# Moving small state-space steps earlier and later around a matmul stream: f and A two blocks ahead, C behind other pairs, scan tables among the W coefficients, one coefficient group behind the scan

## The chip, the cores and the metric

The kernel runs on one core of one Trainium2 chip. The metric is the device time of one execution in microseconds; with it stands the profile of one execution, whose span is the time from the first to the last recorded event of the core.

## The reference

One decoder layer on 512 tokens of width 1024, in float32:

```
h = rms_norm(x) * norm_w
u, z_s, q, k, v, z_a, r_s, r_a = split(h @ w_in)          # w_in: 1024 x 9216
y_s = ((S5(u) glu) * silu(z_s)) @ w_ssm_out               # state-space branch
y_a = (dilated_attention(q, k, v) * silu(z_a)) @ w_attn_out
out = x + (sigmoid(r_s) * y_s + sigmoid(r_a) * y_a) @ w_o
```

The state-space branch has 64 groups of 16 channels with 64 complex states each. Per group, with `dt = exp(log_dt)` and `a = exp(lam * dt)`:

```
f  = (a - 1) / lam ;  bb = f * b
state[t] = a * state[t-1] + bb @ u[t]                     # complex, diagonal
y[t] = Re(c @ state[t]) + d_skip * u[t]
g = gelu(y);  S5 = g * sigmoid(g @ w_glu)
```

## The kernel before

**The matmul stream.** Every large product is done as three matmuls on split operands (high part times high part, high times low, low times high). A weight tile `w_raw` is fetched by a DMA of SyncE's queue (SP), ScalarE (ACT) makes its high part `w_hi` (L250), VectorE (DVE) makes its low part `w_lo` (L252). There are two raw buffers and three of each part, and a tile is prepared two units before it is used. A unit of the projection (`cm_unit`) takes one weight tile of 128 columns: 8 slices of the contraction, 3 matmuls of 128x512 each, so 24 matmuls. Two slices, six matmuls, are one *block*, and each unit of this kind has four blocks.

**The order.** All TensorE (PE) instructions are tied in the order in which the program text traces them. The other engines' queues are filled by the framework's scheduler, which takes instructions as they become ready in its own simulation, those traced first ahead of others; at run time each queue is then strictly in that order. `tc.issue_after(ins)` puts the instructions of its block behind `ins` on their engine's queue.

**Work woven into the stream.** The list `events` names for each small step the block in whose front it is traced. Block 0 is the first of unit u3; W0 = 16, K0B = 49, V0B = 74 and Y0 = 88 are marks in it. The steps, in their order:

- `f_turn` turns `pw` (f in slot 8, a in slot 0, computed on DVE, last written at L543 and L547) onto the partitions by 16 small matmuls into `ftp`. ACT copies them to `fT` (L576) and `AT` (L577). DVE makes f times b (L578 to L581) and doubles the powers of a in `AT` (L590 to L593). GpSimd (POOL) copies the top power to `A4` (L595 to L597).
- `w_unit(j)`, eight of them, three blocks apart from W0: six DVE instructions of `coef` (L422 to L424) fill one of two buffers in the tile `ab`, eight transposes bring it to `wps`, ACT copies that to `W`.
- `x_pair(i)`, four of them, at W0+5, 11, 17 and 23: 64 small matmuls per unit, of `W` with u, into `xps`; ACT copies them into `Xs` (L465, L466), the inputs of all steps of the scan.
- `ca_load(j)`, `ca_turn(j)`, `ca_coef(j)`, for eight chunks: the rows of c are loaded to `cn` (two buffers), turned by eight matmuls into `cps`, copied by ACT to `p3` (L808, L809), and multiplied with the powers of a by six DVE instructions of `coef` into one of three buffers of `ab`.
- `scan_tables` (L717 to L730): 17 DVE instructions that spread `A4` and raise it. `tables_last` traces them behind the last coefficient instruction traced so far.
- The scan, in eleven portions four blocks apart from W0+26: 7 steps with `run_end` and 7 with `step` over the whole of `Xs`, of three DVE instructions each (L737, L741, L742), and between them 7 short carries (L752, L755) and `run_first`. Each step reads what the step before it wrote.
- `m_unit(j)`: 64 matmuls into `kps` from the chunk's coefficients; ACT, POOL and eight POOL DMAs make the matrix M of the chunk.
- `chunk(j)` from Y0 on: `ca_turn(j+3)`, then `y_unit(j)` (32 matmuls with M, 64 with `Xs` and the chunk's coefficients, into `yps`), then `ca_coef(j+3)`, and `make_m(j+2)` (the `kps` matmuls).

Behind this come the gate, the output product of the state-space branch, the attention heads and the last products, which the change does not touch.

Of the kernel before, what the change touches and what calls it, by code (L numbers as in the profile page):

```python
# [11 lines left out]
F32 = mybir.dt.float32  # L12
# [3 lines left out]
ALU = mybir.AluOpType  # L16
# [4 lines left out]
P = 128  # L21
# [6 lines left out]
Q = 16  # L28
# [24 lines left out]
def tile_hybrid_block(ctx: ExitStack, tc: tile.TileContext, x, positions, norm_w, w_in, lam_re, lam_im,  # L53
# [3 lines left out]
    act, dve, pool, sp = nc.scalar, nc.vector, nc.gpsimd, nc.sync  # L57
# [24 lines left out]
    sml = ctx.enter_context(tc.tile_pool(name="sml", bufs=2))  # L82
# [25 lines left out]
    def bank(name):  # L108
        return ps_tile("g", name)
# [4 lines left out]
    def t2k(name, dtype=F32):  # L114
        return tmp.tile([P, 512], dtype, name=name, tag="t2k")
# [290 lines left out]
    def load_u(j, Uj=None):  # L406
        if Uj is None:
            Uj = t2k("Uj")
        sp.dma_start(Uj, ud[j].rearrange("q g s c -> s q g c"))
        return Uj.rearrange("p (g c) -> p g c", g=8)  # L410
# [3 lines left out]
    def coef(dst, p0, a1, a2, n0, n1, t, eng):  # L414

        n, ng = n1 - n0, dst.shape[1]
        sh = [P, ng, n, Q]
        gs = slice(p0, p0 + ng)
        ar = AT[:, 0, gs, n0:n1].unsqueeze(3).broadcast_to(sh)
        ai = AT[:, 1, gs, n0:n1].unsqueeze(3).broadcast_to(sh)  # L420
        tv = t[:, 0:ng * n * Q].rearrange("p (g k q) -> p g k q", g=ng, k=n)
        dve.tensor_tensor(dst, a1.unsqueeze(2).broadcast_to(sh), ar, op=ALU.mult)  # L422
        eng.tensor_tensor(tv, a2.unsqueeze(2).broadcast_to(sh), ai, op=ALU.mult)
        coefs[0] = dve.tensor_tensor(dst, dst, tv, op=ALU.add).ins  # L424
# [25 lines left out]
    sza = cst.tile([P, NP, S], F32, name="sza")  # L450
    early = {}
    Xs = Xsv = None
    W0, K0B, V0B, Y0 = 16, 49, 74, 88
# [149 lines left out]
    def w_next(j):  # L603
        Ws[j] = w_unit(j)
        if j not in early:
            early[j] = load_u(j)
# [125 lines left out]
    def step(dst, prev, x):  # L732

        ta = tas[n_ta[0] % 2]
        n_ta[0] += 1
        sh = [P, 2, 2 * H, NJ]
        dve.tensor_tensor(ta.rearrange("p o a (g j) -> p o (a g) j", j=NJ),  # L737
                          prev.rearrange("p a g j -> p (a g) j").unsqueeze(1).broadcast_to(sh),
                          A4x.rearrange("p o a (g j) -> p o (a g) j", j=NJ), op=ALU.mult)
        tv = ta.rearrange("p o a (g j) -> p o a g j", j=NJ)  # L740
        dve.tensor_tensor(dst, x, tv[:, :, 0], op=ALU.add)  # L741
        dve.tensor_tensor(dst, dst, tv[:, :, 1], op=ALU.add)  # L742

    Ev = E.rearrange("p a (g j) -> p a g j", j=NJ)

    def run_end(i):

        step(Ev, Xs[:, :, :, 1] if i == 1 else Ev, Xs[:, :, :, (i + 1) % NI])
# [15 lines left out]
        with tc.issue_after(coefs[0]):  # L764
            scan_tables()

    scan_work = [tables_last]
    scan_work += [lambda i=i: run_end(i) for i in range(1, NI)]
    scan_work += [lambda j=j: run_carry(j) for j in range(1, NJ)]
    scan_work += [run_first]  # L770
    scan_work += [lambda i=i: step(Xs[:, :, :, i], Xs[:, :, :, i - 1], Xs[:, :, :, i]) for i in range(1, NI)]

    V = new_v()
# [13 lines left out]
    def ca_load(j):  # L787
        cn = sml.tile([P, P], F32, name="cn")
        rows = slice(j * P, (j + 1) * P)
        sp.dma_start(cn[:, 0:64], c_re[0].rearrange("g p n -> (g p) n")[rows])  # L790
        sp.dma_start(cn[:, 64:128], c_im[0].rearrange("g p n -> (g p) n")[rows])
        dg = sml.tile([Q, 8, Q], F32, name="dg", bufs=3)
        sp.dma_start(dg.rearrange("q g p -> q (g p)"), d_skip[0:1, rows].to_broadcast([Q, P]))
        pool.tensor_tensor(dg, dg, ident[0:Q, 0:Q].unsqueeze(1).broadcast_to([Q, 8, Q]), op=ALU.mult)
        cns[j], dgs[j] = cn, dg

    def ca_turn(j):
        cn = cns.pop(j)
        ps = bank("cps")
        for i in range(2):  # L800
            a = 1 - i
            for h in range(2):
                pe.matmul(ps[64 * h:64 * h + 64, 64 * i:64 * i + 64], cn[:, 64 * a:64 * a + 64], idp[:, h],
                          start=True, stop=True, skip_group_check=True)

        p3 = sml.tile([P, 3, 4, Q], F32, name="p3")
        p3f = p3.rearrange("p a g q -> p (a g q)")
        act.copy(p3f[:, 0:64], ps[:, 64:128])  # L808
        act.activation(p3f[:, 64:192], ps[:, 0:128], AF.Copy, scale=-1.0)  # L809
        p3s[j] = p3  # L810

    def ca_coef(j):
        p3 = p3s.pop(j)
        ca = ab[j % 3].rearrange("p (a g k q) -> p a g k q", a=2, g=4, k=9)
        for a in range(2):
            coef(ca[:, a], 4 * j, p3[:, a], p3[:, a + 1], 0, 9, abt[:, 3 * nca:], dve)
        cas[j] = ca

    def m_unit(j, ca, dg):

        kt = big.tile([Q, 8, T, Q], F32, name="kt", tag=("s7a", "s7b")[j % 2])
        ps = [bank("kps") for _ in range(2)]
        for c in range(2):
            for m in range(4):
                for h in range(2):
                    sl = slice(64 * h, 64 * h + 64)
                    pe.matmul(ps[h][32 * m:32 * m + Q, 0:P], BB[sl, 1 + c, 4 * j + m, :], ca[sl, c, m, 1:9, :],
                              start=c == 0, stop=c == 1, skip_group_check=True, tile_position=(64 * h, 32 * m))
        for m in range(4):
            for h in range(2):  # L830
                act.copy(kt[:, 2 * m + h].rearrange("q k p -> q (k p)"), ps[h][32 * m:32 * m + Q, 0:P])
        pool.tensor_tensor(kt[:, :, T - 1, :], kt[:, :, T - 1, :], dg, op=ALU.add)  # L832

        M = Mb[j % 3]
        for t in range(T):
            pool.dma_start(M[Q * t:Q * t + Q, :, 0:P - Q * t], kt[:, :, t:].rearrange("q g k p -> q g (k p)"))  # L836
        return M
# [49 lines left out]
    def make_m(j):  # L887
        Ms[j] = m_unit(j, cas[j], dgs.pop(j))
# [16 lines left out]
    def chunk(j):  # L905
        if j > 0:
            s = y_turn(j - 1)
        if j + 3 < 8:
            ca_turn(j + 3)
        ysbs[j] = y_unit(j, cas[j], Ms.pop(j), Us.pop(j))  # L910
        if j + 3 < 8:
            ca_coef(j + 3)
        if j + 2 < 8:
            make_m(j + 2)
            load_us(j + 2)
        if j > 0:
            gelu(j - 1, s, *gTs)
        if j + 4 < 8:
            ca_load(j + 4)

    def scanning(i, n):
        for f in scan_work[i * len(scan_work) // n:(i + 1) * len(scan_work) // n]:
            f()
# [3 lines left out]
        Xs = big.tile([P, 2, G // 2, NI, NJ], F32, name="Xs", tag="s2")  # L927
        Xsv = Xs.rearrange("p a g i j -> p a g (i j)")

    events = [(3, begin_x), (6, lambda: early.update({3: load_u(3, sza[:, 3])})), (7, f_turn)]  # L930
    events += [(W0 + 3 * j, lambda j=j: w_next(j)) for j in range(8)]
    events += [(W0 + 5 + 6 * i, lambda i=i: x_pair(i)) for i in range(4)]
    for j in range(3):
        events += [(W0 + 11 + 3 * j, lambda j=j: ca_load(j)), (W0 + (17, 17, 23)[j], lambda j=j: ca_turn(j)),
                   (W0 + 25, lambda j=j: ca_coef(j))]
    events += [(W0 + 24, clear_m), (K0B, lambda: make_m(0)), (K0B, lambda: make_m(1)), (K0B, lambda: ca_load(3))]
    events += [(W0 + 26 + 4 * i, lambda i=i: scanning(i, 11)) for i in range(11)]
    events += [(V0B, lambda: fin.pop()()), (Y0 - 10, lambda: load_us(0)), (Y0 - 10, lambda: load_us(1))]
    events += [(Y0 + (11 * j + 1) // 3, lambda j=j: chunk(j)) for j in range(8)] + [(Y0 + 28, lambda: gelu(7, y_turn(7), *gTs))]
    events = sorted(enumerate(events), key=lambda e: (e[1][0], e[0]))  # L940
    events = [e for _, e in events]
# [446 lines left out]
```

## Time and profile before

| | |
|---|---|
| three runs | 681.3 us median (679.34 to 682.19) |
| profiled execution | 681.45 us |
| its span | 679.4 us, mean granted TensorE clock 0.997 |
| PE matmul busy | 668.7 us, 98% |
| PE weight load busy | 565.1 us, 83% |
| DVE busy | 463.7 us, 68% |
| ACT busy | 322.5 us, 47% |
| POOL busy | 115.5 us, 17% |

In the profile's rows a line number is a line of the kernel, `out<-in` are the program's tile names, and a bracket behind a row gives the idle time of that engine just ahead of it and what ended it. A matmul's busy time is longer than the distance to the next one, because matmuls overlap: distances between starts tell the pace. A timeline row stands for one instruction or for several equal ones; its first two numbers are start and length in microseconds.

### The profile page before, as it was taken

What the parts mean: (1) busy time and instruction counts of PE and PEld (TensorE: products, weight loads), DVE (VectorE), ACT (ScalarE), POOL (GpSimd) and SP (SyncE); (2) the same over time, 40 slices, a digit from 0 to 9 for tenths busy, and PEclk for the clock granted to TensorE, in tenths of its full rate; (3) what the DMA queues carried; (4) which work ended last, traced back from release to release, by engine and by line L of the source; (5) the groups of instructions that cost most, each with busy time, mean ns of one, the idle gap of its engine ahead of it and who ended that gap; (6) DMA issues with size and microseconds to landing.
All of it is one profiled execution on the core that took longest, in us unless ns stands there. A gap on an engine that the chain in (4) does not pass through costs nothing.

```text
span 679.4 us, 12601 instructions
## 1 busy us (share of the span) xinstructions
PE 668.7 (98%) x4785; PEld 565.1 (83%) x4785; DVE 463.7 (68%) x965; ACT 322.5 (47%) x676; POOL 115.5 (17%) x273
## 2 busy tenths in 40 slices
PE   8999999999899999999999999999999999999997
PEld 8987888889687888878889888888888888888886
DVE  7979889998688354863238777658665856667531
ACT  6644554323367653441244673556455735733210
POOL 1010000600365418520000030012001200220000
PEclk9999999999899999999999999999999999999999
DMA  9666324643455634473333423222322223247231
GB/s 310 123 164 170 103 82 129 175 141 108 116 134 140 154 122 139 140 247 109 93 94 94 140 62 87 58 76 63 94 71 78 72 61 94 93 141 278 94 123 63
DMA packets 137380, 82.13 MB, mean 121 GB/s; under 512 B 32736, under 2 KB 125928, under 8 KB 137192
## 3 DMA queue, kind: packets, MB, share of 16 engines
q1 hardware_dynamic: 134968, 78.31, 39.0%
q0 software_dynamic: 2048, 2.36, 2.2%
q8 instruction: 38, 0.62, 0.4%
q10 hardware_dynamic: 304, 0.66, 0.3%
q14 instruction: 22, 0.18, 0.1%
HBM read 68.46 MB, written 10.49 MB: 116 GB/s over the span
## 4 chain that ended last, share of the span: by engine, by line
PE 87%; DVE 5%; issue 2%; ACT 2%; DMA 2%; POOL 1%; SPq 0%; ACTq 0%; DVEq 0%; POOLq 0%
PE pj L69 72%; PE sps L69 3%; PE yps L69 2%; PE ot L69 2%; PE ptp L74 2%; DVE w_lo L252 2%; PE qtp L74 2%; ACT w_hi L250 1%; PE xps L69 1%; PE wps L74 1%; DVE gth L1250 1%; PE kps L69 1%; DMA x_all<-in_x_dram 1%; DMA qkw<-in_q_norm_w_dram 1%; PE yT L74 0%
## 5 line engine op out<-in xcount | busy, mean ns | idle before, releaser
L250 ACT ACTIVATE w_hi<-w_raw 128x1024 fp32r<-128x1024 f32 x94 | 99.4, 1058 | 158.5 <-PE pj L69 134.3
L252 DVE TENSOR_TENSOR w_lo<-w_raw,w_hi 128x1024 fp32r<-128x1024 f32 x94 | 118.2, 1259 | 62.1 <-ACT w_hi L250 60.8
L69 PE MATMUL pj<-hT_hi,w_hi 128*128 128x512 f32 (+1 forms) x344 | 132.1, 386 | 0.0
L69 PE MATMUL pj<-hT_lo,w_hi 128*128 128x512 f32 (+1 forms) x344 | 129.3, 378 | 0.4 <-DVE hT_lo L355 0.4
L69 PE MATMUL pj<-hT_hi,w_lo 128*128 128x512 f32 (+1 forms) x344 | 127.2, 377 | 0.0
L69 PE MATMUL pj<-w_hi,hT_hi 128*128 128x512 f32 (+1 forms) x288 | 108.7, 377 | 0.0
L69 PE MATMUL pj<-w_hi,hT_lo 128*128 128x512 f32 (+1 forms) x288 | 105.6, 367 | 0.0
L69 PE MATMUL pj<-w_lo,hT_hi 128*128 128x512 f32 (+1 forms) x288 | 105.5, 366 | 0.0
L69 PEld LDWEIGHTS pj<-hT_hi,w_hi 128*128 128x128 f32 x344 | 65.1, 189 | 12.9 <-issue 1.3
L69 PEld LDWEIGHTS pj<-hT_lo,w_hi 128*128 128x128 f32 x344 | 65.2, 189 | 11.2 <-DVE hT_lo L355 0.6
L69 PEld LDWEIGHTS pj<-hT_hi,w_lo 128*128 128x128 f32 x344 | 64.0, 189 | 12.0
L69 PEld LDWEIGHTS pj<-w_hi,hT_lo 128*128 128x128 f32 x288 | 54.3, 189 | 9.1
L69 PEld LDWEIGHTS pj<-w_hi,hT_hi 128*128 128x128 f32 x288 | 54.4, 189 | 8.5 <-issue 0.5
L69 PEld LDWEIGHTS pj<-w_lo,hT_hi 128*128 128x128 f32 x288 | 54.5, 189 | 7.5
L1112 POOL COPY sw<-st 32x4 f32<-32x4 f32 x64 | 11.8, 185 | 175.0 <-ACT Pt L1068 172.2
L1013 DVE SCALAR_TENSOR_TENSOR qkp<-qtp,wcol,qkp 128x512 fp32r<-128x512 f32 (+1 forms) x32 | 23.6, 748 | 25.3 <-ACT qkp L1012 25.2
L1068 ACT ACTIVATE Pt<-Pt,st 128x256 f32<-128x256 f32 (+1 forms) x64 | 30.9, 484 | 19.8 <-DVE st L1066 19.8
L836 POOL DMA_DIRECT2D dd<-kt x64 | 33.7, 534 | 2.4 <-POOL kt L832 2.1
L1012 ACT ACTIVATE qkp<-qtp,wcol 128x512 fp32r<-128x512 f32 (+1 forms) x32 | 21.2, 682 | 23.1 <-PE qtp L74 20.8
L69 PE MATMUL pj<-w_lo,mT_hi 128*128 128x512 f32 (+1 forms) x72 | 26.3, 366 | 0.0
L69 PE MATMUL pj<-w_hi,mT_hi 128*128 128x512 f32 (+1 forms) x72 | 26.3, 366 | 0.0
L69 PE MATMUL pj<-w_hi,mT_lo 128*128 128x512 f32 (+1 forms) x72 | 26.3, 365 | 0.0
(299 smaller groups left out, 1182.4 us busy)
## 6 DMA issues: line engine op xcount, KB each, us to landing
w_raw<-in_w_in_dram SPq DMA_DIRECT2D x36, 512.0 KB
w_raw<-in_w_in_dram SPq DMA_DIRECT2D x112, 128.0 KB
w_raw<-in_w_glu_dram SPq DMA_DIRECT2D x8, 512.0 KB
w_raw<-in_w_ssm_out_dram SPq DMA_DIRECT2D x8, 512.0 KB
w_raw<-in_w_o_dram SPq DMA_DIRECT2D x8, 512.0 KB
w_early<-in_w_in_dram SPq DMA_DIRECT2D x4, 512.0 KB
ud<-uT SPq DMA_DIRECT2D x8, 256.0 KB
uss<-ud SPq DMA_DIRECT2D x8, 256.0 KB
```

The costliest lines, as they stand in the source:

```text
L69: last[0] = nc.tensor.matmul(*a, **k)
L74: last[0] = nc.tensor.transpose(*a, **k)
L250: last_act[0] = act.activation(hi, raw, AF.Copy).ins
L252: dve.tensor_tensor(lo, raw, hi.bitcast(F32), op=ALU.subtract)
L836: pool.dma_start(M[Q * t:Q * t + Q, :, 0:P - Q * t], kt[:, :, t:].rearrange("q g k p -> q g (k p)"))
L1012: act.activation(hi, ps[sl], AF.Copy, scale=w)
L1013: dve.scalar_tensor_tensor(lo, ps[sl], w, hi.bitcast(F32), op0=ALU.mult, op1=ALU.subtract)
L1068: act.activation(o, o, AF.Exp, bias=nm, scale=-1.0, accum_out=st[:, kind, 1, h, b:b + 1])
L1112: pool.tensor_copy(sw[32 * r:32 * r + 32, :, :, b], st[32 * b:32 * b + 32, 1, :, :, r])
L1250: dve.scalar_tensor_tensor(th, th, 1.0, z, op0=ALU.add, op1=ALU.mult)
```

## The change

1. `f_turn` is traced at block 5 instead of block 7.
2. For the chunks 0, 1, 2: `ca_load` at W0+7, 8, 12 (before: W0+11, 14, 17), `ca_turn` at W0+11, 11, 17 (before: W0+17, 17, 23), so behind the second and third pair of x instead of the third and fourth. `p3` gets a third buffer.
3. `tables_last` is an event of its own at W0+16, behind the coefficients of `w_unit(5)`, where it was the first item of the scan, behind those of `ca_coef(2)`. The scan's list has 22 items instead of 23.
4. `ca_coef(0)` and `ca_coef(1)` stay at W0+25; `ca_coef(2)` moves from there to Y0 and is put on DVE's queue behind the last instruction of the scan (`done[0]`).

```
-        dve.tensor_tensor(dst, dst, tv[:, :, 1], op=ALU.add)
+        done[0] = dve.tensor_tensor(dst, dst, tv[:, :, 1], op=ALU.add).ins
+
+    done = [None]
...
-    scan_work = [tables_last]
+    scan_work = []
...
-        p3 = sml.tile([P, 3, 4, Q], F32, name="p3")
+        p3 = sml.tile([P, 3, 4, Q], F32, name="p3", bufs=3)
...
+    def behind_scan(j):
+        with tc.issue_after(done[0]):
+            ca_coef(j)
...
-    events = [(3, begin_x), (6, lambda: early.update({3: load_u(3, sza[:, 3])})), (7, f_turn)]
+    events = [(3, begin_x), (6, lambda: early.update({3: load_u(3, sza[:, 3])})), (5, f_turn)]
...
-        events += [(W0 + 11 + 3 * j, lambda j=j: ca_load(j)), (W0 + (17, 17, 23)[j], lambda j=j: ca_turn(j)),
-                   (W0 + 25, lambda j=j: ca_coef(j))]
-    events += [(W0 + 24, clear_m), (K0B, lambda: make_m(0)), ...]
+        events += [(W0 + (7, 8, 12)[j], lambda j=j: ca_load(j)), (W0 + (11, 11, 17)[j], lambda j=j: ca_turn(j)),
+                   ((W0 + 25, W0 + 25, Y0)[j], lambda j=j: ca_coef(j) if j < 2 else behind_scan(j))]
+    events += [(W0 + 16, tables_last), (W0 + 24, clear_m), (K0B, lambda: make_m(0)), ...]
```

More of the change, by code (lines that the diff above doesn't have):

```diff
@@ L933, in tile_hybrid_block @@
     for j in range(3):
-        events += [(W0 + 11 + 3 * j, lambda j=j: ca_load(j)), (W0 + (17, 17, 23)[j], lambda j=j: ca_turn(j)),
-                   (W0 + 25, lambda j=j: ca_coef(j))]
-    events += [(W0 + 24, clear_m), (K0B, lambda: make_m(0)), (K0B, lambda: make_m(1)), (K0B, lambda: ca_load(3))]
+        events += [(W0 + (7, 8, 12)[j], lambda j=j: ca_load(j)), (W0 + (11, 11, 17)[j], lambda j=j: ca_turn(j)),
+                   ((W0 + 25, W0 + 25, Y0)[j], lambda j=j: ca_coef(j) if j < 2 else behind_scan(j))]
+    events += [(W0 + 16, tables_last), (W0 + 24, clear_m), (K0B, lambda: make_m(0)), (K0B, lambda: make_m(1)), (K0B, lambda: ca_load(3))]
     events += [(W0 + 26 + 4 * i, lambda i=i: scanning(i, 11)) for i in range(11)]
```

## The prediction

> **What bounds the kernel now.** I read the page's busy table, then PE's waits, then the timelines around the two long ones. First the page and PE's waits:
>
> ```profile
> PE 668.7 (98%) x4785; PEld 565.1 (83%) x4785; DVE 463.7 (68%) x965; ACT 322.5 (47%) x676; POOL 115.5 (17%) x273
> ...
> PE yps L69 <- DVE Xs L742: 2.7, 1, 2.7
> ...
> PE wps L74 <- DVE ab L424: 1.2, 1, 1.2
> ```
>
> PE is the bound: 98% of the span, in an order that is fixed. The change adds and removes no matmul, so it can only move what PE waits for. Two waits stand in the part it touches. PE's timeline at the first (the first transposes of the W coefficients), and at a later place of the same kind without a wait:
>
> ```profile
> 53.12 0.39 PE L69 MATMUL pj<-hT_hi,w_lo 128*128 128x512 f32 x1
> 54.71 1.26 PE L74 MATMUL wps<-ident,ab 128*128 128x128 f32 x8 [1.20 <-DVE ab L424]
> 55.73 0.48 PE L69 MATMUL pj<-hT_hi,w_hi 128*128 128x512 f32 x1
> ...
> 79.09 0.39 PE L69 MATMUL pj<-hT_hi,w_lo 128*128 128x512 f32 x1
> ...
> 80.11 0.48 PE L69 MATMUL pj<-hT_hi,w_hi 128*128 128x512 f32 x1
> ```
>
> From the last big matmul before to the first behind: 55.73 - 53.12 = 2.61 with the wait, 80.11 - 79.09 = 1.02 without. The first wait costs **1.59 us**. The second stands in chunk 0, where the `yps` matmuls need the end of the scan; chunk 1 is the same work without it, from `cps` on:
>
> ```profile
> 172.19 0.45 PE L69 MATMUL cps<-ident,cn 128*64 128x64 f32 x8
> ...
> 176.32 1.16 PE L69 MATMUL yps<-ab,Xs 64*64 64x64 f32 x64 [2.74 <-DVE Xs L742]
> 177.41 0.91 PE L69 MATMUL kps<-ab,dd 64*16 64x128 f32 x32
> 178.25 0.79 PE L69 MATMUL pj<-hT_hi,w_hi 128*128 128x512 f32 x1
> ...
> 181.26 0.39 PE L69 MATMUL pj<-hT_lo,w_hi 128*128 128x512 f32 x1
> ...
> 185.69 0.45 PE L69 MATMUL cps<-ident,cn 128*64 128x64 f32 x8
> ...
> 188.68 0.50 PE L69 MATMUL pj<-hT_hi,w_hi 128*128 128x512 f32 x1
> ...
> 190.39 0.39 PE L69 MATMUL pj<-hT_lo,w_hi 128*128 128x512 f32 x1
> ```
>
> From `cps` to the next big matmul chunk 0 takes 178.25 - 172.19 = 6.06, chunk 1 188.68 - 185.69 = 2.99. That is 3.07 too much. The next seven matmul distances are slow as well: 181.26 - 178.25 = 3.01 against 190.39 - 188.68 = 1.71, another 1.30. The granted clock, by stages (PEclk is the column behind POOL):
>
> ```profile
> 53.50:57.00 3.50, 2.30 (x15) 1.89 (x15) 3.50 (x6) 3.08 (x4) 0.00 (x0) 1.00 0.48 137
> ...
> 178.00:181.00 3.00, 3.00 (x23) 2.17 (x8) 2.93 (x5) 1.85 (x9) 0.53 (x2) 0.50 0.40 114
> ```
>
> The clock was halved for about 3 us behind the 2.74 us wait, and not behind the 1.20 us one. So the second wait costs 3.07 + 1.30 = **4.37 us**, if the half clock is its consequence.
>
> **The change, part by part.** *f and A at block 5.* The steps ahead of the first wait, DVE's rows first, then PE's:
>
> ```profile
> 37.08 0.22 DVE L547 TENSOR_TENSOR pw<-scr 64x64 f32<-64x64 f32 x1
> 37.33 1.23 DVE L252 TENSOR_TENSOR w_lo<-w_raw,w_hi 128x1024 fp32r<-128x1024 f32 x1
> 41.34 1.22 DVE L578 TENSOR_TENSOR ab<-dd,fT 128x1024 f32<-128x1024 f32 x1 [2.78 <-ACT fT L576]
> ...
> 53.97 1.28 DVE L424 TENSOR_TENSOR ab<-ab 128x512 f32<-128x512 f32 x2
> ```
> ```profile
> 37.35 0.39 PE L69 MATMUL pj<-hT_hi,w_lo 128*128 128x512 f32 x1
> ...
> 40.07 0.39 PE L69 MATMUL pj<-hT_hi,w_lo 128*128 128x512 f32 x1
> 40.39 0.65 PE L69 MATMUL ftp<-ident,pw 64*64 64x32 f32 x16
> ```
>
> Two blocks are twelve matmuls, so `ftp` starts as far behind the row at 37.35 as it now starts behind 40.07: at 37.67, 2.72 earlier. Its input `pw` is written at 37.08 + 0.22 = 37.30, so PE does not wait, by 0.37. DVE starts L578 0.95 behind the start of `ftp`, then at 38.62; it is free from 37.33 + 1.23 = 38.56 and sat idle for 2.78, so all of the 2.72 is won. The chain from there to the first L424 pair (53.97) holds two weight low parts in any case. It ends 2.72 earlier, the first of the pair at about 51.9, while PE comes to `wps` 1.2 before 54.71, at 53.5. The wait goes, with 1.6 to spare. Added cost: none, if `pw` stays in time; if a weight low part (1.23) came ahead of its last instructions, PE would wait 0.9 in `ftp`.
>
> *C behind other pairs.* 24 matmuls and 6 ACT copies change places. The loads:
>
> ```profile
> 90.35 0.35 SPq L790 DMA_DIRECT2D cn<-in_c_re_dram  x1
> ...
> 75.81 2.09 PE L69 MATMUL xps<-sza,W 128*64 128x64 f32 x64
> ...
> 88.00 2.09 PE L69 MATMUL xps<-Uj,W 128*64 128x64 f32 x64
> ```
>
> `cn` has two buffers, so only the third chunk's load waits for a turn; it was issued right behind the first turns, which follow the third pair of x (88.00 + 2.09). Now they follow the second pair (75.81 + 2.09 = 77.9), and the third turn follows the third, so 12 us are left for a load of 64 KB. I take 0; if SP's queue, in order, held it behind a weight fetch, PE would wait up to about 2. What is gained is that `p3` is there early: L423 of the chunks 0 and 1 can run in DVE's gaps. ACT's copies, 0.3 each, fall in front of a weight high part that waits for PE anyway: 0.
>
> *Scan tables at W0+16.* They stood directly in front of the scan; now they fall into a gap of DVE:
>
> ```profile
> 79.96 1.29 DVE L422 TENSOR_TENSOR ab<-dd,AT 128x512 f32<-128x512 f32 x2 [1.93 <-PE wps L74]
> ...
> 109.57 0.69 DVE L717 COPY scn<-A 128x1024 f32<-128x1024 f32 x1
> ```
>
> 17 instructions, one of 0.7 and sixteen of about 0.2: between 0.6 + 16 x 0.1 = 2.2 (their spacing) and 3.9 (their durations). The idle 1.93 covers most of it, and that gap is one in which DVE is ahead of PE and waits for its transposes: 0 on PE. Without that cover up to 2 would come on PE.
>
> *Third chunk's coefficients behind the scan, and the scan earlier.* This is the term that decides. The rows of DVE, ACT's last copy into `Xs`, and DVE's groups from 110.4 to 176.3:
>
> ```profile
> 101.97 0.76 DVE L424 TENSOR_TENSOR ab<-ab 128x576 f32<-128x576 f32 x1
> 103.70 0.76 DVE L422 TENSOR_TENSOR ab<-p,AT 128x576 f32<-128x576 f32 x1 [0.97 <-ACT p L808]
> ...
> 106.38 1.22 DVE L252 TENSOR_TENSOR w_lo<-w_raw,w_hi 128x1024 fp32r<-128x1024 f32 x1
> ...
> 110.48 1.22 DVE L737 TENSOR_TENSOR scn<-Xs,scn 128x1024 f32<-128x1024 f32 x1
> ...
> 173.17 1.23 DVE L252 TENSOR_TENSOR w_lo<-w_raw,w_hi 128x1024 fp32r<-128x1024 f32 x1 [0.37 <-ACT w_hi L250]
> ...
> 175.58 0.69 DVE L742 TENSOR_TENSOR Xs<-Xs,scn 128x512 f32<-128x512 f32 x1
> ```
> ```profile
> 103.33 0.22 ACT L466 COPY Xs<-xps 128x32 f32<-128x32 f32 x1
> ```
> ```profile
> L252 DVE TENSOR_TENSOR w_lo<-w_raw,w_hi 128x1024 fp32r<-128x1024 f32 x12 | 14.7, 1222 | 2.1 <-ACT w_hi L250 2.1
> ...
> L621 DVE SCALAR_TENSOR_TENSOR z<-th,pj 128x512 f32<-128x512 f32 x7 | 4.8, 680 | 0.0
> ```
>
> The scan begins when three things are done. `Xs` is complete at 103.55, and 1.59 earlier behind the first gain: 101.96. The chunks 0 and 1 end at 102.73, paced by PE: 101.14. Tables: long done. So it begins at about 102.0, not 110.48. It took 175.58 + 0.69 - 110.48 = 65.8 us, of which 14.7 are twelve weight low parts, 4.8 are seven `z`, 0.8 one coefficient product and 2.1 waits for `w_hi`: 43.4 alone (rests of the tables in it, which go too; not counted). In the new place it meets eleven low parts (13.4) and eight `z` (5.5): 102.0 + 43.4 + 13.4 + 5.5 = 164.3, or 166.4 with the 2.1. PE comes to these `yps` at 176.32 - 2.74 - 1.59 = 171.99. The second wait goes, with 5.6 to 7.7 to spare.
>
> What is late next is `kps` of the third chunk, 177.41 - 176.32 = 1.09 behind: 173.08. It needs the six instructions now behind the scan. Four of them took 106.38 - 103.70 = 2.68, so six take 4.0, or 4.5 by durations; a weight low part of 1.2 falls among them, perhaps two. They end between 164.3 + 4.0 + 1.2 = 169.5 and 166.4 + 4.5 + 2.4 = 173.3. I take no wait, since even the late end is 0.2 off; the cover is at most 3.6 us.
>
> *Sum.* 681.45 - 1.59 - 4.37 = **675.5 us**, against the profiled 681.45 (its span and 2.05 around it), which is 0.15 over the median. Behind chunk 0 PE goes on in its order at the old pace, and nothing there is bound to a clock time, so it keeps the gain.
>
> **Rivals.** *Late coefficients.* DVE's queue is strict, and the row at 173.17 shows a low part that waited for ACT with scan steps queued behind it. If the low part of that unit (then at 173.17 - 1.59 = 171.6, done at 172.8) is queued ahead of three to six of the moved instructions, they end at 174.8 to 176.8, `kps` waits 1.7 to 3.7, and the longer wait brings the half clock again: 677.2 to 680.5, middle 679. Against it: they would be ready some us before.
>
> *The scan is not earlier* (the other side). If DVE's order leaves its start near 110, PE still waits for its end, and the six come on top. It decides when the scan ends later than 177.41 - 4.0 = 173.4, that is, gains under 2.9 us. At a gain of 1.3 (thirteen short table instructions that stood inside the scan, 0.1 each) it ends at 175.0, the six at 179.0 to 180.7, and `kps` is 1.6 to 3.3 late against before: 683.0 to 684.8, about 684. Against it: the four instructions and tables between 103.70 and 110.48 leave for certain.
>
> *f earlier pays nothing*: `pw` is just late, or L424 late by another queue order: 675.5 + 1.6 = 677.1.
>
> *The half clock is not the wait's.* Nothing in the trace but its place ties the two. If it stays: 675.5 + 1.3 = 676.8. The Trainium skill, "TensorE: Matmul & The Clock Gate", section "Part 1: The HAM clock gate", says that the clock falls to half after at least one idle window of about 3.4 us; by that rule a wait of 2.74 us would not do it, and 1.3 would not come back. The trace disagrees as far as it goes, with a clock of 0.50 directly behind the 2.74 us.
>
> **How the numbers follow.** Forecast 0.58 (675.5; by the spread of the runs, -2.0 and +0.9 around their median, 673.5 to 676.4). Late coefficients 0.18 (679), scan not earlier 0.09 (684), f pays nothing 0.07 (677.1), half clock stays 0.08 (676.8). A measurement of this kernel tells about 0.5%, 3.4 us, from no change: faster is under 677.9. Faster 0.58 + 0.07 + 0.08 = 0.73; same 0.18; slower 0.09. The range goes from 673.5 up to the middle of the late coefficients and the spread, 679.6; what it leaves out is the slower rival and a part of the late coefficients, under 2 in 10.
>
> **What the profile after would show.** `ftp` near 37.7 with no wait, and no wait of `wps` for L424. L717 near 76, the first L737 near 102, the last L742 between 163 and 167. The six coefficient instructions behind it, done before `kps`; no wait of `yps` or `kps`, and no stretch with a clock of 0.5 near 177. The prediction is wrong if `kps` waits for `ab`, if the scan starts later than 106, or if `cps` waits for a load of `cn`.

## The result and the profile after

The changed kernel takes 674.93 us (median of 6 runs, 674.39 to 675.61) against 681.68 (6 runs, 679.34 to 682.46): a ratio of 0.9905, 95% interval 0.9888 to 0.9921. Its profiled execution took 675.1 us, span 673.1.

PE's waits in the profile after, without the first (for the identity matrix, as before); the columns are the total, the number and the longest:

```profile
PE kps L69 <- issue: 1.0, 1, 1.0
PE hps L74 <- DVE x_all L336: 0.8, 1, 0.8
PE pj L69 <- DVE hT_lo L355: 0.4, 1, 0.4
```

Both waits that the change could reach are gone (`wps` for L424, `yps` for L742). The waits of `hps` and `pj` stand ahead of anything that it moves; the one of `kps` for "issue" (time in which the profile shows nothing that PE waited for) is in chunk 4 and is not the one that was feared. PE's timeline after, at the two places and with the block of f and A:

```profile
37.70 0.66 PE L69 MATMUL ftp<-ident,pw 64*64 64x32 f32 x16
...
53.15 0.39 PE L69 MATMUL pj<-hT_hi,w_lo 128*128 128x512 f32 x1
53.38 1.03 PE L74 MATMUL wps<-ident,ab 128*128 128x128 f32 x8
54.17 0.48 PE L69 MATMUL pj<-hT_hi,w_hi 128*128 128x512 f32 x1
...
170.59 0.45 PE L69 MATMUL cps<-ident,cn 128*64 128x64 f32 x8
...
171.91 1.16 PE L69 MATMUL yps<-ab,Xs 64*64 64x64 f32 x64
173.00 0.66 PE L69 MATMUL kps<-ab,dd 64*16 64x128 f32 x32
173.59 0.50 PE L69 MATMUL pj<-hT_hi,w_hi 128*128 128x512 f32 x1
...
175.31 0.40 PE L69 MATMUL pj<-hT_lo,w_hi 128*128 128x512 f32 x1
```

The first place takes 54.17 - 53.15 = 1.02, as at the place without a wait before: 1.59 less. `cps` to the next big matmul takes 173.59 - 170.59 = 3.00 instead of 6.06, and the seven distances behind it 1.72 instead of 3.01. DVE's timeline after (its waits in brackets), from which that comes:

```profile
51.03 1.28 DVE L424 TENSOR_TENSOR ab<-ab 128x512 f32<-128x512 f32 x2
...
75.18 0.69 DVE L717 COPY scn<-A 128x1024 f32<-128x1024 f32 x1
...
102.16 1.23 DVE L737 TENSOR_TENSOR scn<-Xs,scn 128x1024 f32<-128x1024 f32 x1 [0.76 <-ACT Xs L465]
...
164.50 0.69 DVE L742 TENSOR_TENSOR Xs<-Xs,scn 128x512 f32<-128x512 f32 x1
165.10 0.75 DVE L422 TENSOR_TENSOR ab<-p,AT 128x576 f32<-128x576 f32 x1
...
169.83 0.76 DVE L424 TENSOR_TENSOR ab<-ab 128x576 f32<-128x576 f32 x1
```

The scan starts at 102.16, waiting for nothing but ACT's last copies into `Xs`. It ends at 165.19, 6.7 ahead of `yps`, and the moved coefficients end at 170.59, 2.4 ahead of `kps`. The granted clock in the window that had 0.50 before:

```profile
178.00:181.00 3.00, 3.00 (x50) 2.50 (x49) 0.76 (x1) 1.83 (x3) 3.00 (x6) 1.00 0.74 134
```

### The profile page after: what moved, and what is told of

Its sections match the earlier page's. It is cut to its first block, busy times and chain, and to the rows that moved or that the text cites. A ratio compares the mean times of both kernels' runs of the same rounds, so it can differ in the third digit from the quotient of the medians.

```text
span 673.1 us, 12602 instructions
## 1 busy us (share of the span) xinstructions
PE 665.6 (99%) x4785; PEld 563.4 (84%) x4785; DVE 463.8 (69%) x965; ACT 322.6 (48%) x676; POOL 116.1 (17%) x273
## 4 chain that ended last, share of the span: by engine, by line
PE 88%; DVE 4%; issue 2%; POOL 2%; ACT 2%; DMA 1%; SPq 0%; ACTq 0%; POOLq 0%; DVEq 0%
PE pj L69 73%; PE sps L69 3%; PE yps L69 2%; PE ot L69 2%; PE ptp L74 2%; PE qtp L74 2%; DVE w_lo L252 1%; PE xps L69 1%; ACT w_hi L250 1%; PE wps L74 1%; DVE gth L1255 1%; DMA x_all<-in_x_dram 1%; PE kps L69 1%; DMA qkw<-in_q_norm_w_dram 1%; PE yT L74 0%
```

## The experiments

Each result is the median, with the ratio to the kernel before on the same chip (681.2 to 681.7 there) and its 95% interval.

**One part undone.** Does each part carry something of its own? Four kernels, each the changed one with one part put back.

```
x1_f_back:      -(5, f_turn)                        +(7, f_turn)
x2_coef_back:   -((W0 + 25, W0 + 25, Y0)[j], ... behind_scan(j))   +(W0 + 25, lambda j=j: ca_coef(j))
x3_tables_back: -events += [(W0 + 16, tables_last), ...             +scan_work = [tables_last]
x4_c_back:      -(W0 + (7, 8, 12)[j], ca_load), (W0 + (11, 11, 17)[j], ca_turn)
                +(W0 + 11 + 3 * j, ca_load), (W0 + (17, 17, 23)[j], ca_turn)
```

> The changed kernel with f_turn at block 7 again, all else as changed. Theory (two separate waits): the first wait is back, 1.59 us between the last big matmul and the first behind wps, and nothing else: 675.1 + 1.6 = 676.7; the end of the scan stays over 5 us ahead of yps. Rival (the earlier f only lets PE arrive earlier at the next wait, so it is worth nothing by itself): 675.1.

677.51 us, 0.995 (0.993 to 0.997). PE's timeline of this kernel at the first place:

```profile
53.20 0.39 PE L69 MATMUL pj<-hT_hi,w_lo 128*128 128x512 f32 x1
54.80 1.26 PE L74 MATMUL wps<-ident,ab 128*128 128x128 f32 x8 [1.22 <-DVE ab L424]
55.81 0.48 PE L69 MATMUL pj<-hT_hi,w_hi 128*128 128x512 f32 x1
```

The same 2.61 as before, and no wait of `yps`. The first part stands by itself. (The time is 0.8 over the expected one, within runs from 676.56 to 680.71.)

> The changed kernel with the third chunk's coefficients at W0+25 again, in front of the scan; C turns and tables stay early. Theory (the scan had 6.7 us to spare, its end at 165.2 against PE's arrival at 171.9): the scan starts up to 4 us later, ends before 169.5, no wait of yps: 675.1, the move of the coefficients bought nothing that the other moves had not bought. Rival (their place is what the gain hangs on): yps waits again, over 677.

675.61 us, 0.9923 (0.9893 to 0.9954): no wait of `yps`, the scan ends at 168.1. The move of the third chunk's coefficients is not needed beside the others.

> The changed kernel with the scan tables as first item of the scan again. Theory: about 0.9 of the tables comes ahead of the first step and 1.3 into the scan, the end of the scan moves from 165.2 to 167.4 and the six coefficient instructions behind it end at 172.8 to 173.0 instead of 170.6; kps comes at 173.0, so between no wait and 0.5: 675.1 to 675.6. Rival (the cover behind the scan is larger than the trace shows, or the tables are needed early): 675.1 with the coefficients well ahead, or over 677 with a wait of yps.

675.35 us, 0.992 (0.9894 to 0.9945): the scan starts at 102.53 and ends at 166.1, and the six end at 171.5, better than the 172.8 expected. The rests of the tables mostly fit between the dependent steps: with three of them in between, the first step's second instruction starts 1.44 behind its first (102.53 to 103.97), in the changed kernel without them 1.26. Not needed either.

> The changed kernel with the loads and turns of C for the chunks 0 to 2 at their old places (W0+11, 14, 17 and W0+17, 17, 23). Theory: the coefficients of the chunks 0 and 1 are paced by PE (their buffers come free with the last W transposes), not by p3, so they end at about 101.4 as now, the scan starts near 102: 675.1, and the C turns bought nothing beside the others. Rival (the early p3 is what frees DVE in front of the scan): the scan starts some 2 us later and kps begins to wait, 676 or more.

676.68 us, 0.9927 (0.9905 to 0.995), with runs from 674.77 to 679.14. The scan starts at 102.10, as in the changed kernel, and PE waits for DVE neither at `yps` nor at `kps`: the C turns are not needed beside the others. The profiled run has more waits for "issue" (1.2 at `kps`, 0.3 at `yps`); whether that, or anything, makes it 1 us slower than its neighbours stays open, as the intervals overlap.

**One part alone.** If each of the three scan parts can be left out, which of them are enough? The kernel before with one part of the change (the same diffs, the other way round).

> The kernel before with f_turn at block 5 as the only change. Theory: the first wait goes (1.59); the start of the scan is tied to PE (the third C turn follows the last pair of x), so it and PE's arrival at yps both come 1.59 earlier, and the wait of yps stays 2.7 with its half clock: 681.4 - 1.6 = 679.8. Rival (the scan's end is fixed by DVE's own work): the 1.59 is handed on to the wait of yps, 681.4.

679.76 us, 0.998 (0.9966 to 0.9995): 1.4 faster. The wait of `yps` is 2.74 as before, only earlier, with a half clock behind it, so the gain of the first part is not handed on to it.

> The kernel before with only the scan tables moved to W0+16. Theory: the scan starts 0.9 earlier and holds 1.3 less, so it ends 2.2 earlier, and the wait of yps shrinks from 2.74 to 0.5; a wait that short leaves the clock alone, so the 1.3 of the half clock goes too: 681.4 - 2.2 - 1.3 = 677.9. Rival (the half clock is not the wait's): 679.2.

677.40 us, 0.9948 (0.9933 to 0.9964). There is no wait of `yps` at all, where 0.5 was expected. DVE's timeline of this kernel says why:

```profile
101.80 0.76 DVE L424 TENSOR_TENSOR ab<-ab 128x576 f32<-128x576 f32 x1
...
103.32 1.22 DVE L737 TENSOR_TENSOR scn<-Xs,scn 128x1024 f32<-128x1024 f32 x1 [0.76 <-ACT Xs L465]
104.47 0.75 DVE L422 TENSOR_TENSOR ab<-p,AT 128x576 f32<-128x576 f32 x1
```

The scan starts at 103.3 and not at 109.6, with the third chunk's coefficients behind its first step. So in the kernel before the tables were the gate: `tables_last` put them behind the last of those coefficients, and the first step needs them.

> The kernel before with only the third chunk's coefficients moved behind the scan (p3 has its third buffer). Theory, the rival of late coefficients as it would be without the other moves: the scan starts 4 to 5 earlier than 110.5 and ends near 172, ahead of yps at 173.6, but the six instructions and a weight low part come behind it and end near 177, so kps, due at 174.7, waits about 2.5: 681.4 - 4.4 + 2.5 = 679.5, or 680.8 with the half clock. Rival (kps is hidden): 677.0.

677.47 us, 0.9946 (0.9931 to 0.9961). The rival holds. The timelines of DVE and PE in this kernel:

```profile
166.85 0.69 DVE L742 TENSOR_TENSOR Xs<-Xs,scn 128x512 f32<-128x512 f32 x1
...
172.18 0.76 DVE L424 TENSOR_TENSOR ab<-ab 128x576 f32<-128x576 f32 x1
```
```profile
173.54 1.16 PE L69 MATMUL yps<-ab,Xs 64*64 64x64 f32 x64
174.63 0.66 PE L69 MATMUL kps<-ab,dd 64*16 64x128 f32 x32
```

The scan ends at 167.5, not near 172: it starts at 103.7, 6.8 earlier than before and not 4 to 5. The coefficients are done 1.7 ahead of `kps`.

> The kernel before with only the loads and turns of C for the chunks 0 to 2 moved forward (p3 has its third buffer). Theory: with p3 early, the third chunk's coefficients fill DVE's gaps between 88 and 98 instead of standing behind the last pair of x, and the scan starts about 4 earlier; no wait of yps is left: 681.4 - 4.4 = 677.0, the whole of the second gain from this part alone. Rival (they stay in their order behind the second chunk's, which is paced by the last W transposes): the scan starts at most 1 us earlier, 680.4 or more.

677.34 us, 0.9949 (0.9929 to 0.9969). The time is as expected, the way is not: here the scan starts only at 108.84, 1.6 earlier. DVE's timeline at its end:

```profile
171.64 0.69 DVE L742 TENSOR_TENSOR Xs<-Xs,scn 128x512 f32<-128x512 f32 x1
173.23 1.23 DVE L252 TENSOR_TENSOR w_lo<-w_raw,w_hi 128x1024 fp32r<-128x1024 f32 x1 [0.90 <-ACT w_hi L250]
```

It ends at 172.33, 3.9 earlier. In the kernel before, the low part at 173.17, its wait for ACT and a coefficient product (L423) stood between the scan's last steps; now they are behind its end. So this part leaves the tables where they were, behind the third chunk's coefficients, and wins by another way: 1.6 at the start and the rest by what DVE's queue has between the last steps. Each of the three parts alone removes the whole second wait.

**The size of a wait, and what it does to the clock.** Instructions that change no value are added to the scan's chain, `n` = 6, 7 and 10 of them with the coefficients at W0+25 (y), and 6 in the changed kernel as it is (k):

```
     def run_first():
+        for _ in range(n):
+            dve.tensor_tensor(E, E, E, op=ALU.max)
         S0 = Xs[:, :, :, 0]
```

> A wait of yps made to measure: the changed kernel with the third chunk's coefficients back at W0+25 (so that nothing stands behind the scan), and six added instructions of 0.72 in the scan's chain, which take the maximum of E with itself and change no value. The scan's end moves from 168.2 to 172.5, or 173.6 if a weight low part falls in; PE is at yps at 172.1: a wait of 0.4 to 1.5. Theory (the half clock of the kernel before was the consequence of its 2.74 wait, and a wait of about 1.2 does not bring it): clock 1.00 behind it, 675.6 + 0.4 to 1.5 = 676.0 to 677.1. Rival (any wait at this place brings it): 1.3 more.

> The same with seven added instructions: the scan's end at 173.2 to 174.4, a wait of 1.1 to 2.3. Theory: the clock halves somewhere between a wait of 1.2 and one of 2.74, so this is 676.7 to 677.9 with a full clock or 678.0 to 679.2 with the half one. By the rule of the Trainium skill, 'TensorE: Matmul & The Clock Gate' (a window of about 3.4 us of idleness), the clock stays at 1.00.

> The same with ten added instructions: the scan's end at 175.4 to 176.5, a wait of 3.3 to 4.4. Theory: half clock behind it for about 3 us, 675.6 + 3.3 to 4.4 + 1.3 = 680.2 to 681.3. Rival (the slow stretch of the kernel before was not the wait's): no half clock, 678.9 to 680.0.

679.84 (0.9971, 0.9956 to 0.9987), 681.73 (0.9994, 0.9979 to 1.0009) and 683.65 us (1.0025, 1.0006 to 1.0044). All three waits came out longer than meant: 3.1, 4.0 and 5.8, because the scan's end moved by more than what was added (with six instructions, 4.3 us, by 7.2: from 168.1 to 175.3). So all three times lie above their ranges, none of the waits is a short one, and the question between 1.2 and 2.74 was not answered by them. PE's wait with `n` = 6, 7 and 10:

```profile
PE yps L69 <- DVE Xs L742: 3.1, 1, 3.1
...
PE yps L69 <- DVE Xs L742: 4.0, 1, 4.0
...
PE yps L69 <- DVE Xs L742: 5.8, 1, 5.8
```

The granted clock by stages of 2 us (the third number from the end), in the same order:

```profile
174.00:176.00 2.00, 0.60 (x25) 0.60 (x28) 1.31 (x3) 0.00 (x0) 0.00 (x0) 0.88 0.51 150
176.00:178.00 2.00, 2.00 (x83) 1.68 (x76) 0.86 (x2) 0.65 (x2) 0.00 (x0) 0.50 1.00 266
178.00:180.00 2.00, 2.00 (x22) 1.49 (x7) 1.97 (x3) 1.51 (x8) 0.00 (x0) 0.76 0.27 82
```
```profile
176.00:178.00 2.00, 2.00 (x88) 1.84 (x96) 0.56 (x1) 0.36 (x2) 0.00 (x0) 0.59 0.99 269
178.00:180.00 2.00, 2.00 (x28) 1.36 (x13) 1.97 (x4) 1.51 (x8) 0.00 (x0) 0.55 0.04 9
```
```profile
174.00:176.00 2.00, 0.00 (x0) 0.00 (x0) 1.93 (x4) 0.00 (x0) 0.00 (x0) 0.84 0.46 113
176.00:178.00 2.00, 0.00 (x0) 0.00 (x0) 1.93 (x3) 0.00 (x0) 0.00 (x0) 0.50 1.03 275
178.00:180.00 2.00, 1.82 (x64) 1.80 (x64) 0.12 (x1) 0.00 (x0) 0.00 (x0) 0.50 0.08 25
180.00:182.00 2.00, 2.00 (x42) 1.36 (x35) 1.98 (x3) 1.33 (x6) 0.00 (x0) 0.50 0.03 8
182.00:184.00 2.00, 2.00 (x9) 1.57 (x9) 1.63 (x3) 0.98 (x5) 0.92 (x1) 0.95 0.00 0
```

In each of these profiles the half clock comes with the long wait. A mean of 0.88 over 2 us is 0.48 us at half: with `n` = 6 the half clock lasted 0.48 + 2.0 + 0.96 = 3.4 us, with 7 1.64 + 1.80 = 3.4, with 10 0.64 + 6.0 + 0.20 = 6.8.

> The changed kernel as it is, third chunk's coefficients behind the scan, with the same six added instructions of 0.72 in the scan's chain. The scan's end moves from 165.2 to 169.5, still ahead of yps at 171.9, and the six coefficient instructions, with a weight low part among them, end near 174.7 instead of 170.6. Theory (the cover behind the scan is what kps leaves, 173.0 - 170.6 = 2.4): kps waits about 1.7, 675.1 + 1.7 = 676.8. Rival (kps does not wait for the last of them, or the cover is larger): 675.1.

683.13 us, 1.0012 (0.9995 to 1.0028): no faster than before, 6.3 more than expected. PE's waits in this kernel, and its timeline and DVE's:

```profile
PE kps L69 <- DVE ab L424: 3.0, 2, 1.5
...
PE yps L69 <- DVE Xs L742: 1.5, 1, 1.5
```
```profile
173.53 1.16 PE L69 MATMUL yps<-ab,Xs 64*64 64x64 f32 x64 [1.47 <-DVE Xs L742]
176.21 0.66 PE L69 MATMUL kps<-ab,dd 64*16 64x128 f32 x16 [1.51 <-DVE ab L424]
178.33 0.66 PE L69 MATMUL kps<-ab,dd 64*16 64x128 f32 x16 [1.47 <-DVE ab L424]
```
```profile
171.65 1.23 DVE L252 TENSOR_TENSOR w_lo<-w_raw,w_hi 128x1024 fp32r<-128x1024 f32 x1 [0.67 <-ACT w_hi L250]
172.79 0.69 DVE L742 TENSOR_TENSOR Xs<-Xs,scn 128x512 f32<-128x512 f32 x1
```

4.3 us of added work moved the scan's end by 8.3, from 165.2 to 173.5. The low part at 171.65 and its 0.67 of waiting now stand ahead of the scan's last instruction; in the changed kernel they are behind it. In all the scan now meets thirteen low parts, not eleven (2.4 us more), and 2.8 us of waiting for `w_hi`, not 1.4. The coefficients of the third chunk follow, mixed with those of the next, and `kps` waits for each half of them. This is the wait that the rival of late coefficients had, but `yps` waits as well, which it had not.

## Why the prediction was right

The time (675.5 forecast, 674.93 measured) and the steps agree. The gain is 6.75 between the medians, 0.8 more than the 5.96 of the sum, which is within the spread of the runs.

- *f and A.* `ftp` at 37.70 (37.67 forecast), the first L424 from 51.03, about 51.7 at its end (51.9), and the wait gone for 1.59. With this part undone its wait is back; alone it gave 1.4.
- *The second wait.* Forecast 3.07 + 1.30; measured 6.06 - 3.00 = 3.06 and 3.01 - 1.72 = 1.29.
- *The scan.* Start 102.16 (102.0), end 165.19 (164.3 to 166.4), coefficients done at 170.59 (169.5 to 173.3), `yps` 171.91 (171.99), `kps` 173.00 (173.08). The row that carried it was that of ACT's last copies into `Xs`, which the first step waited for.
- *What costs nothing.* The tables took their place among the W coefficients from 75.18 on, and no `cps` waited for a load.
- *The half clock is the wait's.* The rival with 676.8 is refuted: the clock is 1.00 where the wait is gone, and 0.50 where the added instructions bring it back. Of 62 executions of the eight kernels without the wait, 60 have a mean granted clock of 0.999 or 1.000; of 77 of the kernel before, 26.

Three things were less right than the number. I called the third chunk's coefficients the term that decides and priced the tables and the C turns at 0; the runs show three parts of which each alone takes away all of the second wait (677.4, 677.5, 677.3), so none of them decides beside the others, and undoing any one of them left no such wait. I put the rival of late coefficients at 679 by its low part alone; `k6_late_coefs`, the kernel with the six added instructions and the coefficients behind the scan, is at 683, as there the low parts delay the scan as well, so 4.3 us of added work were enough for a time no better than before. And the parts 3.07 and 1.30 are not quite the wait and the half clock: `kps` before took 178.25 - 177.41 = 0.84 where chunk 1 takes 0.58, so 0.26 of the 3.07 belongs to the half clock as well. The sum stays 4.37.

The profiled executions differ by 6.35, the sum by 5.96. By PE's starts the shift is 5.98 at chunk 1 (188.68 to 182.70) and 6.34 at the last matmuls, so the rest came behind the change, from waits that differ from run to run: the first matmuls of the product behind the gate waited 0.2 for ACT and 0.2 for DVE before and not after (0.7 in their starts), and `kps` waited longer for "issue" after, which takes 0.3 off again (0.7 before, 1.0 after, 0.7 to 1.2 in the experiments).

## What to carry to other kernels

Price a wait by the distance between its fixed neighbours on the bounding engine, and add the slow stretch behind it: here 2.74 us of waiting cost 4.37 in the profiled execution. Before adding up several edits that serve one wait, look for what gates the start of the chain in question. One edge (the tables behind the last coefficients) held the scan here; two of the edits let go of it, the third left it and made the scan start 1.6 earlier, with less other work between its last steps, and each was enough alone. A chain that becomes longer on a shared queue also meets more of the other work there, so a margin is smaller than it looks: 4.3 us of added work became 8.3.

## What the runs showed of the hardware

The half clock comes in pieces of about 3.4 us, not in proportion to the wait: 3.4 for a wait of 2.74 (the kernel before, and `o1_f_alone`, which is the kernel before with `f_turn` at block 5), of 3.14 (`n` = 6) and of 4.00 (`n` = 7), twice that for 5.85 (`n` = 10). In `k6_late_coefs` it came too, for 6.8 us, with no single wait over 1.51. The granted clock by stages, first of that kernel, then of `o1_f_alone`:

```profile
174.00:176.00 2.00, 0.69 (x48) 0.55 (x40) 2.00 (x4) 0.65 (x2) 0.00 (x0) 0.98 0.59 134
176.00:178.00 2.00, 0.66 (x16) 0.17 (x16) 1.97 (x4) 0.00 (x0) 0.00 (x0) 0.50 0.94 259
178.00:180.00 2.00, 1.67 (x19) 1.06 (x20) 1.97 (x4) 0.86 (x5) 0.00 (x0) 0.50 0.04 8
180.00:182.00 2.00, 2.00 (x6) 1.59 (x5) 1.93 (x3) 0.81 (x4) 0.81 (x2) 0.50 0.00 0
182.00:184.00 2.00, 2.00 (x8) 1.59 (x7) 0.13 (x1) 0.00 (x0) 2.00 (x5) 0.81 0.45 66
```
```profile
176.00:178.00 2.00, 2.00 (x35) 1.41 (x28) 2.00 (x3) 1.84 (x8) 0.00 (x0) 0.56 1.03 284
178.00:180.00 2.00, 2.00 (x7) 1.55 (x6) 1.65 (x2) 0.47 (x3) 1.15 (x3) 0.58 0.13 38
```

In `k6_late_coefs` it begins 0.08 before 176.00. In the 3.4 us ahead of that, PE waited from 172.5 to 173.53 and from 174.70 to 176.21 less 0.3, 2.2 us or about two thirds. Worked out in this way the share is about 60% in the kernel before (waiting from 174.3 to 176.32, half clock from 177.68) and 57% in `o1_f_alone` (waiting from 172.85 to 174.79, half clock from 176.25). So, as an estimate from these runs, what counts is the idle share of such a piece of time, and 57% is enough. The lower limit is not shown: behind the first wait of the kernel before, at most 1.6 us idle, the clock stayed at 1.00, but that wait may have been divided between two pieces. The Trainium skill, "TensorE: Matmul & The Clock Gate", section "Part 1: The HAM clock gate", gives a window of 3.4 us, and the length of the pieces agrees; it lets the clock fall after at least one idle window, and the pieces of 60% and 57% were not idle throughout.

Nor does the same kernel have the half clock every time. One piece of 3.4 us takes 0.25% off the mean granted clock of an execution. Of the 77 executions of the kernel before, on three chips, 26 have 0.999 or 1.000, so no whole piece, with a median of 680.5 us; 39 have 0.996 or 0.997, with 681.7. That difference of 1.2 is of the size of what the trace gave (1.30, or 1.56 with `kps`). With `n` = 6 it is 3 executions of 12 without a piece, with `n` = 7 and 10 and in `k6_late_coefs` none. What decides it was not traced. The half clock began 1.36 us behind the end of the wait in the kernel before, 1.46 in `o1_f_alone`, 0.42 with `n` = 7 and 0.12 with `n` = 6, so it does not start at a fixed distance from the wait. That the pieces lie differently against the wait from one execution to the next would fit, but is not shown.
